# A decay chain split in two, three input products on VectorE, and new due times for the state space steps of a hybrid S5 and retention encoder

## The chip, the cores and the metric

The kernel runs on one core of a Trainium2 chip. The metric is the device time of one execution in microseconds (us); the kernel before takes 1299.02 us, the median of 3 runs (1296.56 to 1300.02).

## The reference, cut to what matters

One encoder layer is applied to two request groups, 512 and 256 positions, with 16 learned meta positions in front of each. After an RMS norm, one projection gives the inputs of two branches:

- Branch A, the state space branch (S5). For each of 2 directions, 32 groups and 64 complex states, `ab = exp(lam * dt)` is the step factor, `bb = (ab - 1) / lam * b` are the scaled input weights, `s_t = ab * s_{t-1} + bb * u_t` is the scan over positions, and `y = Re(c * s) + d * u`, then GELU and a gated projection.
- Branch B, retention with 4 heads. Its decay per head comes from `log_sigmoid(ret_decay_logit)`, 8 numbers in all, from which tables of powers of the decay are made.

The branches are merged by gates, projected and added; a second RMS norm, a gated feed-forward layer and a final RMS norm follow. The output is 512 and 256 rows of 1024.

## The kernel before, in words

**Tiling.** The 768 positions are 6 row tiles of 128, the meta positions a small seventh. Weights are split into a high and a low part (`convert`, L161: ScalarE copies the high part, `tt(eng, lo, ...)` on VectorE or POOL subtracts it), and each product is three matmuls (`mm3`, L79). Weight tiles 3 to 11 have their low parts made on POOL, the others on VectorE (L215).

**Order.** Between L590 and L1733 the order of the instructions on each engine is the order in which the program issues them. An instruction that waits holds up all that follows on its engine; the DMA queue is SyncE's (SP).

**The front (L740 to L785).** Row by row: mean square on ScalarE, `rstd_of` on POOL, `scale_row` on VectorE (L622), 8 transposes on TensorE (`to_features`, L631), high and low part (`n1_hi` on ScalarE, `n1_lo` on VectorE, L641 to L650). `u_block` (L681) projects a quarter of the S5 input for half the positions in 24 matmuls. In this row of calls stands `decay_params()` (L698 to L732, called at L775), the log-sigmoid of the 8 decays as a chain of tiny POOL operations (128x8) with one VectorE reciprocal in the middle (L718), and then `dcols` (L732), the factors that the retention tables need. `s5_params` (L435) is a generator of VectorE steps for `ab`, its powers and the scaled inputs `Bb` (`inputs`, L525 to L549, half of it three POOL operations, L541 to L543); `step(n)` runs n of them. `step(N0)` runs 11 near the start, `step(1000)` (L785) the rest.

**The lanes (L826 to L1080, L1284).** The rest of branch A is five generators:

- `e_lane`: `gbank` (L798) makes 4 groups' input matrices in 6 VectorE operations of 128x512, TensorE transposes them, multiplies by the input (L859), and ScalarE and VectorE (L863) copy the result to `X`. It works on 8 blocks, two events each, with the transposes of a block one event ahead.
- `scan_lane` (L868): 64 steps of 3 VectorE operations on `X`.
- `table_lane` (L898): for 8 blocks, `gbank` on POOL, 16 small TensorE products with `bm` (L933), and DMAs to DRAM.
- `y_lane` (L941): loads the tables, then (second event) runs whatever is left of the scan, copies `X` to `sy`, and in 9 further events does 12 matmuls per block (L985 to L987) and the GELU (L999 to L1004: ScalarE, VectorE, ScalarE, VectorE), then DMAs to DRAM.
- `ret_tables` (the retention tables) and `sums_lane` (sums of the normed input on POOL and VectorE).

**Due times.** The lanes are run between the matmuls of the plain projections (`plain_units`, L1482). The planner's clock (L1094) starts at 0 before the first of them; each piece yields its length in units: 1.92 for 12 matmuls of a `kq_unit` (L1424, 8 units of 4 pieces, to 61.44) and 1.28 for a `v_block` (L1441, 3 units of 14 pieces, to 115.2). After a piece, `passed` runs every event that is due:

```python
    events = deque(sorted(
        spread("e", *E_T, 16) + spread("r", *R_T, 64) + [(t, "s") for t in S_T] + spread("x", *X_T, 24)
        + [(T_FREE, "free")] + spread("c", T_FREE + 0.1, C_DT, 12) + spread("y", *Y_T, 12), key=lambda e: e[0]))
```

`E_T` is the start and spacing of the 16 input events, `R_T` of the 64 scan events, `S_T` the ten table events, `Y_T` the start and spacing of the output events. `v_unit` takes two weight halves before its first and two before its third piece, and each taking issues the conversion of two more (`ws.ahead = 2`, `Ops.two`).

**The end (L2347 to L2374).** Three groups of matmuls finish the lower row tiles 3, 4 and 5. After each, VectorE adds the result to `hres` (`accumulate`), `second_half` takes the mean square on ScalarE and `rstd_from` makes the scale on POOL, and `finish(i, r)` (L2272) writes two 128x512 outputs on VectorE and issues their DMAs. `finish(3)` stands after the addition of tile 4, ahead of that of tile 5.

Of the kernel before, what the change touches and what calls it, by code (L numbers as in the profile page):

```python
# [46 lines left out]
VLP = (0, 1, 2)  # L47
SEQ = 'B Z0 A D KS VM F V0 KL QD F C F F V1 F V2 KT S2 F F KU ST QL KR F F O2 S1 VL F Z2 F QU S0 O1 QR F DL Z1 QS F O0 F ZL'
HALF = 3.84
E_T = (1.9, 0.72)  # L50
R_T = (13.5, 0.997)
X_T = (45, 1.361)
S_T = (2.0, 4.8, 7.6, 10.4, 14, 20, 27, 34, 41, 48)
T_FREE = 82.607
C_DT = 2.446
Y_T = (73, 3.91)
N0 = 11


def build(nc, tc, I, O):  # L60
# [26 lines left out]
    def tt(e, out, a, b, op):  # L87
        e.tensor_tensor(out=out, in0=a, in1=b, op=op)  # L88
# [346 lines left out]
    def s5_params():  # L435
        V.memset(pw[:, 0, 0, :], 1.0)
        V.memset(pw[:, 1, 0, :], 0.0)
        dt = tmp()
        V.tensor_copy(out=dt, in_=prm[:, 2, :])
        yield  # L440
        yield from pexp(dt, G)
        lr, li = prm[:, 0, :], prm[:, 1, :]
        mag, den, dn = tmp(), tmp(), tmp()
        sincos = []

        def magnitude():
            tt(V, mag, lr, dt, MUL)
            yield
            yield from pexp(mag, G)

        def angle():
            th, k1, kf, r, zz = tmp(), tmp(), tmp(), tmp(), tmp()
            c1 = 6.28125
            c2 = 0.0019340515136718750
            c3 = 2 * math.pi - c1 - c2
            yield from chain(
                lambda: tt(V, th, li, dt, MUL),
                lambda: ts(V, k1, th, 1.0 / (2 * math.pi), MUL, MAGIC, ADD),
                lambda: ts(V, kf, k1, -MAGIC, ADD),
                lambda: stt(r, kf, -c1, th, MUL, ADD),  # L460
                lambda: stt(r, kf, -c2, r, MUL, ADD),
                lambda: stt(r, kf, -c3, r, MUL, ADD),
                lambda: ts(V, r, r, 0.25, MUL),
                lambda: tt(V, zz, r, r, MUL))
            sn, cs = tmp(), tmp()

            def sine():
                ts(V, sn, zz, 1.0 / 362880, MUL)
                yield
                for c in (-1.0 / 5040, 1.0 / 120, -1.0 / 6):  # L470
                    stt(sn, sn, c, zz, ADD, MUL)
                    yield
                stt(sn, sn, 1.0, r, ADD, MUL)
                yield

            def cosine():
                ts(V, cs, zz, -1.0 / 3628800, MUL)
                yield
                for c in (1.0 / 40320, -1.0 / 720, 1.0 / 24, -0.5):
                    stt(cs, cs, c, zz, ADD, MUL)  # L480
                    yield
                ts(V, cs, cs, 1.0, ADD)
                yield

            yield from together(sine(), cosine())
            for _ in range(2):
                s2, c2t = tmp(), tmp()
                yield from chain(
                    lambda: tt(V, c2t, sn, sn, MUL),
                    lambda: stt(s2, sn, 2.0, cs, MUL, MUL),  # L490
                    lambda: ts(V, c2t, c2t, -2.0, MUL, 1.0, ADD))
                sn, cs = s2, c2t
            sincos.extend((sn, cs))

        def denominator():
            yield from chain(
                lambda: tt(V, den, lr, lr, MUL),
                lambda: tt(V, dn, li, li, MUL),
                lambda: tt(V, den, den, dn, ADD),
                lambda: V.reciprocal(out=den, in_=den))  # L500

        yield from together(angle(), magnitude(), denominator())
        sn, cs = sincos
        tt(V, pw[:, 0, 1, :], mag, cs, MUL)
        yield
        tt(V, pw[:, 1, 1, :], mag, sn, MUL)
        yield

        def powers():
            for st, n in ((1, 1), (2, 2), (4, 4)):  # L510
                ts_ = [x0.tile([128, 4, G], F32, name="pq", tag="pq", bufs=4)[:, :n] for _ in range(4)]
                ar = pw[:, 0, st:st + 1, :].to_broadcast([128, n, G])
                ai_ = pw[:, 1, st:st + 1, :].to_broadcast([128, n, G])
                xr, xi = pw[:, 0, 1:1 + n, :], pw[:, 1, 1:1 + n, :]
                for t, a, b in zip(ts_, (xr, xi, xr, xi), (ar, ai_, ai_, ar)):
                    tt(V, t, a, b, MUL)
                    yield
                tt(V, pw[:, 0, st + 1:st + 1 + n, :], ts_[0], ts_[1], SUB)
                yield
                tt(V, pw[:, 1, st + 1:st + 1 + n, :], ts_[2], ts_[3], ADD)  # L520
                yield

        bts = [x0.tile([128, G, 16], F32, name="bt", tag="bt", bufs=2) for _ in range(2)]

        def inputs():  # L525
            t1, t2, t3, t4, cr, ci, nr = (tmp() for _ in range(7))
            ai = pw[:, 1, 1, :]
            yield from chain(
                lambda: ts(V, nr, pw[:, 0, 1, :], -1.0, ADD),
                lambda: tt(V, t2, ai, li, MUL),  # L530
                lambda: tt(V, t3, ai, lr, MUL),
                lambda: tt(V, t1, nr, lr, MUL),
                lambda: tt(V, t4, nr, li, MUL),
                lambda: tt(V, t1, t1, t2, ADD),
                lambda: tt(V, t3, t3, t4, SUB),
                lambda: tt(V, cr, t1, den, MUL),
                lambda: tt(V, ci, t3, den, MUL))
            crb = cr[:, :, None].to_broadcast([128, G, 16])
            cib = ci[:, :, None].to_broadcast([128, G, 16])
            br, bi = braw[:, 0], braw[:, 1]  # L540
            tt(P, Bb[:, 0], br, crb, MUL)  # L541
            tt(P, bts[0], bi, cib, MUL)
            tt(P, Bb[:, 0], Bb[:, 0], bts[0], SUB)  # L543
            tt(V, Bb[:, 1], bi, crb, MUL)
            yield
            tt(V, bts[1], br, cib, MUL)
            yield
            tt(V, Bb[:, 1], Bb[:, 1], bts[1], ADD)
            yield  # L549

        yield from together(inputs(), powers())
        nonlocal sc, pwE
        sc = single()
        pwE = sc.rearrange("p (r t g) -> p r t g", r=2, t=8)
        for ri in range(2):
            V.tensor_copy(out=pwE[0:64, ri], in_=pw[0:64, ri, 7::-1, :])
            yield
            V.tensor_copy(out=pwE[64:128, ri], in_=pw[64:128, ri, 0:8, :])
            yield
# [138 lines left out]
    def decay_params():  # L698
        w = [x0.tile([128, 8], F32, name=f"dp{i}") for i in range(4)]
        e, x, y, z = w  # L700
        k = x0.tile([128, 8], I32, name="dpk")
        ts(V, e, dlg, -1.0, MUL)
        tt(V, e, e, dlg, ALU.min)
        ts(P, e, e, -87.0, ALU.max)
        ts(P, x, e, 1.4426950408889634, MUL, MAGIC, ADD)
        ts(P, x, x, -MAGIC, ADD)
        for c in (-0.693359375, 2.12194440e-4):
            ts(P, y, x, c, MUL)
            tt(P, e, e, y, ADD)
        ts(P, y, e, 1.0 / 5040, MUL)  # L710
        for c in (1.0 / 720, 1.0 / 120, 1.0 / 24, 1.0 / 6, 0.5, 1.0):
            ts(P, y, y, c, ADD)
            tt(P, y, y, e, MUL)
        ts(P, k, x, 127.0, ADD, 8388608.0, MUL)
        ts(P, y, y, 1.0, ADD)
        tt(P, e, y, k.bitcast(F32), MUL)
        ts(P, z, e, 2.0, ADD)
        V.reciprocal(out=z, in_=z)  # L718
        tt(P, z, z, e, MUL)
        tt(P, x, z, z, MUL)  # L720
        ts(P, y, x, 1.0 / 17, MUL)
        for c in (15, 13, 11, 9, 7, 5, 3):
            ts(P, y, y, 1.0 / c, ADD)
            tt(P, y, y, x, MUL)
        ts(P, y, y, 1.0, ADD)
        tt(P, y, y, z, MUL)
        ts(P, y, y, -2.0, MUL)
        ts(P, x, dlg, 0.0, ALU.min)
        tt(P, lgc, y, x, ADD)
        lf, lb = lgc[:, 0:4], lgc[:, 4:8]  # L730
        for j, (src, c) in enumerate(((lf, 1.0), (lf, -1.0), (lf, 255.0), (lb, 1.0), (lb, -1.0), (lb, 256.0))):
            ts(P, dcols[:, j, :], src, c, MUL)  # L732

    params = s5_params()

    def step(n):
        for _ in range(n):
            next(params, None)
# [33 lines left out]
    scale_row(5)  # L772
    row_scale(6)
    scale_row(6)
    decay_params()  # L775
    u_block(2, 0)
    to_features(5)
    n1_hi(5)
# [3 lines left out]
    n1_lo(6)  # L782
    u_block(0, 1)
    uws[3] = ws.two()
    step(1000)  # L785
    leave(x0_cm)
    s5_cm = pool("s5")
# [1232 lines left out]
    def h21(i):  # L2020
        return hres[:, 3 + i, 0:512]
# [329 lines left out]
    for i in range(3):  # L2351
# [10 lines left out]
            finish(0, rs[0], qs=(1,))  # L2362
            finish(2, rs[2])
        if i == 1:
            finish(3, rs[3])
            tt(V, h22(2), h22(2), gfin[:, 512:], MUL)
        elif i == 2:
            tt(V, h21(2), h21(2), gfin[:, 0:512], MUL)
            finish(4, rs[4])
    yo = [row_tile() for _ in range(2)]  # L2370
# [106 lines left out]
```

## Time and profile before

| | |
|---|---|
| median of 3 runs | 1299.02 us (1296.56 to 1300.02) |
| the profiled execution | 1295.07 us |
| its span, first to last instruction | 1293.3 us |
| TensorE (PE) busy | 1207.2 us, 93% |
| VectorE (DVE) busy | 917.6 us, 71% |
| POOL busy | 680.6 us, 53% |
| ScalarE (ACT) busy | 594.2 us, 46% |
| granted TensorE clock, mean | 0.974 |
| DMA moved | 155.32 MB, queues 38.4% |

The span is 1.8 us shorter than the profiled execution, which is 3.95 us below the median. Busy shares are means over the whole program. [...]

### The profile page before, as it was taken

How to read it: one execution, taken by the hardware profiler on the slowest of the kernel's cores; microseconds unless marked ns; L12 is line 12 of the kernel's file. 1: busy time of each engine (PE TensorE's matmuls, PEld its weight loads, DVE VectorE, ACT ScalarE, POOL GpSimd, SP SyncE). 2: the span in 40 equal slices, each digit the busy share in tenths (PEclk: the TensorE clock that was granted, in tenths of full speed). 3: DMA queues.
4: the chain of work that ended last, by engine and by line, in shares of the span. 5: the costliest groups of instructions: out<-in, count | busy, mean ns of one | idle time of the engine just before them, and what ended most of it. 6: DMA issues, size and time to landing. Idle time of an engine off the chain costs nothing. (4 is left out here: it accounts for less than half of the span.)

```text
span 1293.3 us, 19211 instructions
## 1 busy us (share of the span) xinstructions
PE 1207.2 (93%) x6821; PEld 1136.7 (88%) x6821; DVE 917.6 (71%) x1514; ACT 594.2 (46%) x1242; POOL 680.6 (53%) x687
## 2 busy tenths in 40 slices
PE   7689998997998999987899997999999999999996
PEld 7688998997988989976899887999999999888884
DVE  6766996658787777887644349766666565899897
ACT  5256343634444444443433245344444444568564
POOL 4777842656676655466355028444444444564174
PEclk9889998999999999998999999999999999999998
DMA  6253456665464435244332600433322222614002
GB/s 248 50 130 100 131 185 181 157 186 168 145 200 137 148 117 182 79 149 159 126 115 74 211 17 33 125 120 94 103 90 66 79 69 78 223 66 152 12 1 97
DMA packets 76734, 155.32 MB, mean 120 GB/s; under 512 B 18000, under 2 KB 37584, under 8 KB 76640
## 3 DMA queue, kind: packets, MB, share of 16 engines
q1 hardware_dynamic: 76640, 154.11, 38.4%
q8 instruction: 53, 0.87, 0.3%
q14 instruction: 41, 0.34, 0.1%
HBM read 118.50 MB, written 35.59 MB: 119 GB/s over the span
## 5 line engine op out<-in xcount | busy, mean ns | idle before, releaser
L88 DVE TENSOR_TENSOR wlo<-wraw,whi 128x512 fp32r<-128x512 f32 x286 | 238.0, 840 | 105.3 <-ACT whi L100 105.0
L100 ACT ACTIVATE whi<-wraw 128x512 fp32r<-128x512 f32 x304 | 183.6, 623 | 46.7 <-POOL wraw L88 14.6
L88 POOL TENSOR_TENSOR wraw<-wraw 128x512 f32<-128x512 f32 x93 | 130.3, 1401 | 141.4 <-DVE wlo L88 94.6
L88 POOL TENSOR_TENSOR wraw<-wrax,wraw 128x512 f32<-128x512 f32 x38 | 51.2, 1346 | 77.4 <-DVE wlo L88 43.7
L82 PE MATMUL bank<-n1hi,wlo 128*128 128x384 f32 x192 | 66.7, 347 | 2.2 <-DVE wlo L88 2.2
L100 ACT ACTIVATE q<-bank 128x384 f32<-128x384 f32 x80 | 38.2, 484 | 66.4 <-PE bank L82 62.3
L80 PE MATMUL bank<-n1hi,whi 128*128 128x384 f32 x192 | 67.6, 352 | 0.0
L81 PE MATMUL bank<-n1lo,whi 128*128 128x384 f32 x192 | 66.4, 346 | 0.0
L80 PE MATMUL pair<-n1hi,whi 128*128 128x384 f32 (+1 forms) x168 | 61.2, 364 | 2.4 <-ACT sgst L100 2.4
L81 PE MATMUL pair<-n1lo,whi 128*128 128x384 f32 (+1 forms) x168 | 59.1, 352 | 0.0
L82 PE MATMUL pair<-n1hi,wlo 128*128 128x384 f32 (+1 forms) x168 | 59.0, 351 | 0.0
L2309 PE MATMUL acc<-whi,ahi 128*128 128x512 f32 x132 | 52.3, 396 | 0.8 <-DVE hres L88 0.8
L88 DVE TENSOR_TENSOR wlo<-wrax,whi 128x512 fp32r<-128x512 f32 x46 | 39.1, 854 | 19.3 <-ACT whi L100 19.3
L2309 PE MATMUL acc<-whi,alo 128*128 128x512 f32 x132 | 52.2, 396 | 0.0
L2309 PE MATMUL acc<-wlo,ahi 128*128 128x512 f32 x132 | 52.2, 395 | 0.0
L88 DVE TENSOR_TENSOR X<-X,single 128x128 f32<-128x128 f32 (+2 forms) x128 | 43.1, 337 | 4.4
L88 POOL TENSOR_TENSOR fr<-fr 128x384 f32<-128x384 f32 x29 | 36.2, 1253 | 13.4 <-DVE alo L88 12.9
L82 PE MATMUL bank<-yThi,wlo 128*128 128x384 f32 x128 | 43.0, 336 | 0.0
L81 PE MATMUL bank<-yTlo,whi 128*128 128x384 f32 x128 | 43.0, 336 | 0.0
L80 PE MATMUL bank<-yThi,whi 128*128 128x384 f32 x128 | 43.0, 336 | 0.0
L80 PE MATMUL pair<-whi,n1hi 128*128 128x256 f32 x144 | 41.7, 290 | 0.0
L94 POOL TENSOR_SCALAR rvar<-ss 128x1 f32<-128x1 f32 (+1 forms) x13 | 5.1, 396 | 68.6 <-ACT nx L100 68.5
(526 smaller groups left out, 4313.1 us busy)
## 6 DMA issues: line engine op xcount, KB each, us to landing
wraw<-in_wfi SPq DMA_DIRECT2D x35, 512.0 KB, 3.7
wraw<-in_win SPq DMA_DIRECT2D x33, 512.0 KB, 5.4
w<-in_wfo SPq DMA_DIRECT2D x16, 512.0 KB, 5.4
wrax<-in_win SPq DMA_DIRECT2D x11, 512.0 KB, 4.3
wrax<-in_wfi SPq DMA_DIRECT2D x11, 512.0 KB, 3.7
fb<-fbscr SPq DMA_DIRECT2D x8, 512.0 KB, 5.0
wraw<-in_wo SPq DMA_DIRECT2D x8, 512.0 KB, 3.6
ffscr<-fr SPq DMA_DIRECT2D x10, 384.0 KB, 2.9
```

The costliest lines, as they stand in the source:

```text
L80: T.matmul(out, l[0], r[0], start=start, stop=False)
L81: T.matmul(out, l[0], r[1], start=False, stop=False)
L82: T.matmul(out, l[1], r[0], start=False, stop=stop)
L88: e.tensor_tensor(out=out, in0=a, in1=b, op=op)
L94: e.tensor_scalar(out=out, in0=a, scalar1=s1, scalar2=s2, op0=op0, op1=op1)
L100: A.activation(out=out, in_=a, func=f, **kw)
L2309: T.matmul(ps, l[a], r[b], start=False, stop=False, skip_group_check=True)
```

## The change

It does four things. `decay_params` becomes a generator of two parts: the first ends before the reciprocal and stays at its place in the front; the second, with the reciprocal, follows after 62 more steps of `s5_params`, behind the first products of all four input quarters' weights. The three POOL operations of `inputs` go to VectorE, each a step of the generator. The due times of the input, scan, table and output events change: input spacing 0.72 to 1.0 units, scan start 13.5 to 18.0, tables further apart up to 57 instead of 48, output start 73 to 81.5 and spacing 3.91 to 2.8. `finish(3)` moves behind the addition of row tile 5.

```diff
-E_T = (1.9, 0.72)
-R_T = (13.5, 0.997)
+E_T = (1.9, 1.0)
+R_T = (18.0, 0.99)
 X_T = (45, 1.361)
-S_T = (2.0, 4.8, 7.6, 10.4, 14, 20, 27, 34, 41, 48)
+S_T = (2.0, 7, 13, 19.5, 26, 32.5, 39, 45.5, 52, 57)
 T_FREE = 82.607
 C_DT = 2.446
-Y_T = (73, 3.91)
+Y_T = (81.5, 2.8)
 N0 = 11
+N1 = 62
...
             br, bi = braw[:, 0], braw[:, 1]
-            tt(P, Bb[:, 0], br, crb, MUL)
-            tt(P, bts[0], bi, cib, MUL)
-            tt(P, Bb[:, 0], Bb[:, 0], bts[0], SUB)
+            tt(V, Bb[:, 0], br, crb, MUL)
+            yield
+            tt(V, bts[0], bi, cib, MUL)
+            yield
+            tt(V, Bb[:, 0], Bb[:, 0], bts[0], SUB)
+            yield
             tt(V, Bb[:, 1], bi, crb, MUL)
...
         ts(P, z, e, 2.0, ADD)
+        yield
         V.reciprocal(out=z, in_=z)
...
             ts(P, dcols[:, j, :], src, c, MUL)
+        yield
 
     params = s5_params()
+    rates = decay_params()
...
     scale_row(6)
-    decay_params()
+    next(rates)
     u_block(2, 0)
...
     u_block(0, 1)
     uws[3] = ws.two()
+    step(N1)
+    next(rates)
     step(1000)
...
         if i == 1:
-            finish(3, rs[3])
             tt(V, h22(2), h22(2), gfin[:, 512:], MUL)
         elif i == 2:
+            finish(3, rs[3])
             tt(V, h21(2), h21(2), gfin[:, 0:512], MUL)
             finish(4, rs[4])
```

## Rows read from the trace of the kernel before

**Rows 1.** Waits of PE, whole span: total us, times, longest.

```profile
PE single L638 <- DVE n1lo L88: 8.0, 1, 8.0
PE single L85 <- ACT sy L100: 4.7, 1, 4.7
PE single L832 <- DVE X L863: 2.5, 1, 2.5
PE single L832 <- ACT ks L100: 1.1, 2, 0.6
```

**Rows 2.** Timeline of DVE, 33 to 63 us: start us, us, instruction [idle before].

```profile
40.83 0.20 DVE L718 RECIPROCAL dp<-dp 128x8 f32<-128x8 f32 x1 [7.40 <-POOL dp L92]
...
49.47 1.29 DVE L88 TENSOR_TENSOR pt<-pt,prm 128x32 f32<-128x32 f32 x1
...
53.00 0.68 DVE L88 TENSOR_TENSOR Bb<-braw,pt 128x512 f32<-128x512 f32 x1
...
54.47 1.54 DVE L88 TENSOR_TENSOR Bb<-Bb,bt 128x512 f32<-128x512 f32 x1
...
62.48 0.69 DVE L88 TENSOR_TENSOR er<-er,tm 128x512 f32<-128x512 f32 x1
```

**Rows 3.** Timeline of PE, 41 to 66 us.

```profile
43.01 0.54 PE L82 MATMUL pair<-n1hi,wlo 128*128 128x400 f32 x1
...
47.34 0.48 PE L80 MATMUL pair<-n1hi,whi 128*128 128x400 f32 x1
...
63.23 0.66 PE L832 MATMUL single<-ident,er 128*128 128x128 f32 x4 [1.05 <-DVE er L88]
65.24 1.09 PE L832 MATMUL single<-ident,ei 128*128 128x128 f32 x4 [1.35 <-DVE ei L88]
```

**Rows 4.** Timeline of POOL, 47 to 56 us.

```profile
47.97 1.46 POOL L92 TENSOR_SCALAR dcols<-lgc 128x4 f32<-128x4 f32 x6
49.40 2.61 POOL L88 TENSOR_TENSOR wlo<-wrax,whi 128x512 fp32r<-128x512 f32 x2
52.78 2.69 POOL L88 TENSOR_TENSOR Bb<-braw,pt 128x512 f32<-128x512 f32 x1 [0.78 <-DVE pt L88]
```

**Rows 5.** Timeline of PE: twelve matmuls between two starts; first output product.

```profile
115.92 0.42 PE L80 MATMUL pair<-n1hi,whi 128*128 128x384 f32 x1
...
118.12 1.92 PE L85 MATMUL single<-Vt,et 128*128 128x99 f32 x16
...
214.82 1.15 PE L85 MATMUL single<-sy,fb 128*128 128x97 f32 x4 [4.74 <-ACT sy L100]
```

**Rows 6.** Stretches: us, PE busy (x) and the other engines, PEclk, DMA, GB/s.

```profile
81.70:85.10 3.40, 3.40 (x13) 3.37 (x11) 3.19 (x6) 1.20 (x3) 3.32 (x4) 0.51 1.11 244
...
214.80:222.00 7.20, 7.17 (x35) 7.18 (x35) 3.30 (x8) 4.53 (x8) 0.00 (x0) 0.53 0.59 174
```

**Rows 7.** Stretch 110 to 113 us, PE instructions with bm alone: busy (x), PEclk.

```profile
110.00:113.00 3.00, 2.16 (x16) 1.00 0.00 0
```

**Rows 8.** Timeline of DVE: first and last scan step.

```profile
121.35 0.40 DVE L88 TENSOR_TENSOR single<-X,single 64x128 f32<-64x128 f32 x1
...
212.67 0.57 DVE L88 TENSOR_TENSOR X<-X,single 128x64 f32<-128x64 f32 x2
```

**Rows 9.** Groups of DVE, 121.3 to 213.3 us: busy, mean ns, idle before.

```profile
L88 DVE TENSOR_TENSOR wlo<-wraw,whi 128x512 fp32r<-128x512 f32 x6 | 4.8, 835 | 0.0
L88 DVE TENSOR_TENSOR ks<-ks,Dg 16x64 f32<-16x64 f32 x6 | 3.8, 628 | 0.2
```

**Rows 10.** Stretch 222 to 262 us: PE, PEld, DVE, ACT, POOL busy, PEclk.

```profile
222.00:262.00 40.00, 40.00 (x348) 39.86 (x347) 23.39 (x41) 24.29 (x44) 22.84 (x21) 1.00 0.70 180
```

**Rows 11.** Timelines of DVE and POOL at the end.

```profile
1284.58 0.68 DVE L88 TENSOR_TENSOR hres<-acc,hres 128x512 f32<-128x512 f32 x1
...
1284.97 0.27 POOL L94 TENSOR_SCALAR rstd<-rtmp,rstd 128x1 f32<-128x1 f32 x1
1286.17 0.76 POOL L94 TENSOR_SCALAR rvar<-fss 128x1 f32<-128x1 f32 x1 [0.93 <-ACT yo L100]
```

## The prediction

> **What bounds the kernel now.** The span is 1293.3 us and PE is busy for 93% of it, so I read the waits of PE first: the reader is to see how short they are beside the span, and that those of 8.0, 4.7 and 2.5 us lead to code that the change touches [rows 1]. Then I looked up, in the timelines of the engine named, why it was late.
>
> The largest, 8.0 us, is one wait for a low part `n1lo`. VectorE stood 7.40 us before the reciprocal of `decay_params`, because POOL was working through the tiny operations ahead of it [rows 2]; the `n1lo` behind it were ready to run, and PE needed them. PE paid twice: after the wait its clock was at the lower level. From 43.01 to 47.34 us 13 matmuls start 0.333 us apart [rows 3]; at the full clock twelve take 2.20 us, 0.183 each [rows 5]. Sixteen at the slow pace cost another 2.4 us. The same is seen after the wait of 2.5 us (the stretch at clock 0.51) and after that of 4.7 us (0.53) [rows 6].
>
> Later VectorE bounds: its scan runs from 121.35 to 213.24 us [rows 8] almost without a gap, with only 6 `wlo` and 6 `ks` operations (8.6 us) between the steps [rows 9], and PE stands 4.7 us for the `sy` copied from its result [rows 1].
>
> **The change, part by part.**
>
> *Decay chain.* VectorE no longer waits at its old place, so `n1lo` and all behind it come about 7.5 us earlier (the wait and the reciprocal's issue), and PE gets the wait of 8.0 and the 2.4 us back: 10.4 us at the end of the next four projections. The reciprocal, 62 steps further, waits for nothing: POOL ends the first part at about 40.8 us as before, VectorE arrives some 3 us after that. The second part on POOL, up to `dcols` at 47.97+1.46 [rows 4], some 8 us, moves to about 44 to 53 us; what it gives is needed at unit 45. Queued behind it on POOL are the low parts of the fifth weight tile (55 us), needed near 64: that slack covers it; without it the price would be those 8 us.
>
> *Inputs on VectorE.* Three operations of 0.68 us [rows 2], 0.65 to the next start: 1.9 us more on VectorE. They take away three POOL operations beside which VectorE was held: its `Bb` operation took 1.54 us beside POOL's of 2.69, 0.86 more than the 0.68 alone [rows 2, 4]. I count 0.86 for each of the three, 2.6 us. The step chain so ends 7.5 - 1.9 - 0.1 + 2.6 = 8.1 us earlier. Against that, POOL's two conversions (2.61 us [rows 4]) now fall beside `gbank` of the first block. Bounds: nothing, as in `er<-er,tm`, 0.69 us beside POOL's scaling of `Cc` [rows 2]; or 1.1 us for each of its two operations with both inputs in SBUF, as for the `pt` operation that took 1.29 beside the same conversions [rows 2, 4] where its neighbours take 0.18. I take 0.7, nearer to the row of the same size and kind.
> [...]
>
> *What is late next.* PE must wait for `er` and `ei` before the fourth quarter's second half: 1.05 and 1.35 us now [rows 3]. PE comes 10.4 us earlier, they come 8.1 - 0.7 = 7.4 earlier, so this wait grows by 3.0. The front is worth 7.4 us, less 0.8 for a slow stretch about twice as long as the 0.9 us that the six slow matmuls there cost now: **6.6 us**, between 5.1 (2.2 for contention) and 8.1.
>
> *Input events.* At 0.72 units three of them came due after one piece: transposes, products, transposes; the second transposes found their PSUM banks not yet copied out (2.5 us [rows 1]), and the slow clock after it cost half of 3.4 us [rows 6]. At 1.0 units it is one pair per 12 matmuls. The two `ks` waits (1.1 us [rows 1]) go to wider table spacing. Of 5.3 us I leave 1.0: **4.3 us**, between 0 and 5.3.
>
> *Scan, tables and outputs.* All due before unit 81.92 (16 input events, the table products) is the same work for PE in another order, so PE reaches it 6.6 + 4.3 = 10.9 us earlier, at 199.2 us where it was at 210.1 (214.82 less the wait of 4.74 [rows 5]). The last input event moves from unit 13.44 to 17.28: two groups of 12 matmuls more before it (4.4 us [rows 5]), one table set less (2.16 us [rows 7]). The scan therefore begins 10.9 - 2.2 = 8.7 us earlier, at 112.65. The third and fourth weight halves of the second `v_unit` are converted in VectorE's queue behind 62 of the 64 steps, since the scan now ends at unit 80.4 and these are issued at 79.36. Before, the scan's 91.9 us lay ahead of them; now 91.9 - 2.1 (two steps) + 0.6 (one more `ks` [rows 9]) + 0.7 (the first half): the first low part is there at 203.7. PE needs it at 199.2: a wait of 4.5 us for `wlo` takes the place of the 4.7 us for `sy`, with the same slow clock. By the time `sy` is due (unit 88.32, 7.7 us of PE work later) it is ready. **0**, between +8.1 (no wait, no slow clock: 4.7 and half of 7.2) and -2.
>
> *Output events* come every 2.8 units, about 5.9 us with their products, for 6.9 before. PE had no wait there; ScalarE was busy 24.29 of 40 us and VectorE 23.39 [rows 10], 70% at the new pace. 0, down to -4. On SP's queue the table and output DMAs move past weight loads issued several pieces ahead of their use: covered by that lead, else the price is a `wlo` wait as above.
>
> *End.* The addition of tile 5 starts at 1284.58 [rows 11] behind `finish(3)`. Now it runs as soon as PE's last product is there, but POOL is in the scale of tile 4 until 1285.24, so tile 5's starts there instead of at 1286.17 [rows 11]: **0.9 us**, between 0 and 1.4. `finish(3)` and its two DMAs fit in VectorE's and SP's idle time before the last scale.
>
> **Sum.** 6.6 + 4.3 + 0 + 0 + 0.9 = 11.8 us. The profiled execution (1295.07 us) would take 1283.3. It lies 3.95 us below the median of 1299.02, which I take as the base: 1287.2.
>
> **Rivals.**
> 1. *POOL holds up the front.* The contention term at its full 2.2 and the `ks`/PSUM waits back (0 instead of 4.3): 5.1 + 0.9 = 6, 1293. For: the 1.29 us row. Against: `er<-er,tm`. It differs from the forecast in the wait for `ei`. Chance 0.14. [...]
> 2. *The wait at 81.92 goes too.* If VectorE is a few us faster, PE needs no `wlo` wait and keeps its clock: up to 8.1 more, 1279. For: VectorE is the only cause; against: the count above. 0.14.
> 3. *The output events become the bound, and it is slower.* A GELU passes ScalarE, VectorE, ScalarE, VectorE in order beside the `sy` copies, sums and weights. If that chain can't be done in 5.9 us, each of the 8 spacings of L1004 falls back to 6.9 (8 us) and PE's clock drops after each wait, as behind all waits over 2 us here: half of 3.4 us, 8 times, 13.6. Net 11.8 - 21.6 = 9.8 slower, 1309. It decides from 2 us of lag per event on. Against: 70% busy. 0.08.
> 4. *It comes to nothing:* VectorE stays the bound through the scan, and the earlier front only makes PE wait longer at 81.92: 1298. This needs the scan to begin no earlier, and [rows 8] show it starting right behind the last input event. 0.09.
>
> **How the numbers follow.** The forecast has 0.55 and gives 1287.2. 1279 to 1296.5 takes in rivals 1 and 2 and leaves out rival 3 and most of 4, some 2 in 10 with the forecast's own edges; the forecast's own range is 1283 to 1292. The limit of 0.3% is 3.9 us, about what a measurement can tell. Faster: forecast, rival 2 and most of 1, 0.81; the same: the rest of 1 and most of 4, 0.11; slower: 0.08.
>
> **What would show it.** Right: no `n1lo` wait over 1 us and clock 1.0 from 35 to 50 us; waits for `er`, `ei` of some 4 and 1.4 us near 52 to 58; no 2.5 us wait at L832 later; the scan beginning near 112; a wait for `wlo` near 199 and none for `sy`; the last addition of a row tile some 10 us before the span's end (8.7 now). Wrong: waits of PE between 205 and 255 us (rival 3), a scan beginning after 116 (rivals 1, 4), or a new wait after 280 us, where nothing was changed.

## The result, and the profile after

The kernel after takes 1281.95 us, the median of 4 runs (1278.82 to 1285.09); the kernel before, run beside it, 1297.79 us (1290.01 to 1300.02). The ratio is 0.9889, with a 95% interval of 0.9839 to 0.9938: 14 us faster, between 8 and 21. The forecast was 1287.2, in a range of 1279.0 to 1296.5. Medians take in every run; the ratios of this document leave out two executions far above all others, 1439.1 us of the kernel before and 4111.85 us of h_both.

| | before | after |
|---|---|---|
| the profiled execution | 1295.07 us | 1285.09 us |
| its span | 1293.3 us | 1283.1 us |
| PE busy | 1207.2 us, 93% | 1206.8 us, 94% |
| VectorE busy | 917.6 us, 71% | 915.6 us, 71% |
| POOL busy | 680.6 us, 53% | 675.5 us, 53% |
| granted TensorE clock, mean | 0.974 | 0.973 |

PE does the same work; what changed is what it waits for. Lines in the kernel after stand 1 to 9 higher than before (the transposes of the lanes are at L841, `X` is copied at L872, `tt` at L89). First the waits of PE in the kernel after, 20 to 260 us, to be held against [rows 1] (total us, times, longest):

```profile
PE pair L82 <- DVE wlo L89: 3.9, 1, 3.9
...
PE single L86 <- ACT ks L101: 2.1, 1, 2.1
...
PE single L841 <- DVE er L89: 0.9, 1, 0.9
PE single L642 <- DVE n1lo L89: 0.4, 1, 0.4
```

The waits of 8.0 us for `n1lo`, 4.7 for `sy` and 2.5 for `X` are gone or below 0.5. Two have come in: 3.9 us for `wlo` and 2.1 us for `ks`; this `ks` wait is another than the two of [rows 1], which stood before transposes and are gone. The places, in the timeline of PE in the kernel after (start us, us, instruction, idle time before and what ended it), which answers to [rows 3] and [rows 5]:

```profile
35.61 0.39 PE L642 MATMUL single<-ident,nx 16*128 16x16 f32 x4 [0.70 <-DVE dp L93]
...
56.94 0.65 PE L841 MATMUL single<-ident,er 128*128 128x128 f32 x4 [0.86 <-DVE er L89]
58.95 1.09 PE L841 MATMUL single<-ident,ei 128*128 128x128 f32 x4 [1.36 <-DVE ei L89]
...
86.25 0.72 PE L86 MATMUL single<-fr,bm 128*48 128x144 f32 x2 [2.10 <-ACT ks L101]
...
207.11 0.58 PE L82 MATMUL pair<-wlo,n1hi 128*128 128x256 f32 x1 [3.90 <-DVE wlo L89]
```

The first row is the landmark of all that follows: the transposes of the first meta tile. The code up to it is the same in all kernels, yet the twelve profiles reach it between 33.16 and 35.61 us (33.30 in that of before, 35.61 here), so stages are compared by the time from there. **A** is the time from the landmark to the transposes of `ei`, the end of the front: 58.95 - 35.61 = 23.34 us, against 31.94 before. **B** is the time from the landmark to the first product named `bank<-whi,n1hi`, which is issued when the due events are over (274.37 us in the profile of before, 265.95 in that of after): 230.34 us, against 241.07.

The timeline of VectorE in the kernel after shows what became of [rows 2] and [rows 8]:

```profile
43.56 1.29 DVE L89 TENSOR_TENSOR pq<-pw 128x32 f32<-128x32 f32 x1
44.78 1.33 DVE L89 TENSOR_TENSOR pt<-pw,prm 128x32 f32<-128x32 f32 x1
...
46.95 0.19 DVE L723 RECIPROCAL dp<-dp 128x8 f32<-128x8 f32 x1
...
56.19 0.69 DVE L89 TENSOR_TENSOR er<-er,tm 128x512 f32<-128x512 f32 x1
...
60.04 1.01 DVE L89 TENSOR_TENSOR er<-er,tm 128x512 f32<-128x512 f32 x1
...
115.68 0.39 DVE L89 TENSOR_TENSOR single<-X,single 64x128 f32<-64x128 f32 x1
...
206.38 1.28 DVE L89 TENSOR_TENSOR wlo<-wrax,whi 128x512 fp32r<-128x512 f32 x2
...
1271.98 0.68 DVE L89 TENSOR_TENSOR hres<-acc,hres 128x512 f32<-128x512 f32 x1
...
1278.86 0.48 DVE L93 TENSOR_SCALAR yq<-hres,rstd 128x512 f32<-128x512 f32 x1 [0.93 <-POOL rstd L95]
```

The reciprocal waits for nothing, where it stood 7.40 us. Row seven is the low part that PE stands for at 207.11, still behind VectorE's scan steps; row eight is the addition of tile 4. And POOL in the kernel after, which answers to [rows 4]:

```profile
43.50 2.56 POOL L89 TENSOR_TENSOR wlo<-wrax,whi 128x512 fp32r<-128x512 f32 x2
47.22 0.28 POOL L89 TENSOR_TENSOR dp<-dp,dp 128x8 f32<-128x8 f32 x1 [1.16 <-DVE pt L89]
...
50.08 0.69 POOL L93 TENSOR_SCALAR dp<-dp 128x8 f32<-128x8 f32 x1
...
53.58 0.23 POOL L93 TENSOR_SCALAR dp<-dp 128x8 f32<-128x8 f32 x1
...
57.35 1.90 POOL L93 TENSOR_SCALAR dcols<-lgc 128x4 f32<-128x4 f32 x6
59.23 2.96 POOL L89 TENSOR_TENSOR wlo<-wraw,whi 128x512 fp32r<-128x512 f32 x2
```

The second part of the decay chain runs from 47.22 to 59.25 us. Its operations of eight columns take 0.69 us beside VectorE's `Bb` and `bt`, which have 512 columns and both inputs in SBUF, and 0.23 later, also beside `er<-single,Bb` (from 54.87 us), which has 512 columns too but one input in PSUM.

Last, stretches of the kernel after (us, PE, PEld, VectorE, ScalarE, POOL busy, granted clock, DMA, GB/s), against [rows 6]. The granted clock is 1.00 or 0.50 at every moment of both profiles, and 0.50 is the lower clock of this text. Behind each of the two new waits PE is at it:

```profile
86.10:89.50 3.40, 3.25 (x12) 2.63 (x13) 2.95 (x5) 1.15 (x4) 0.88 (x2) 0.52 0.00 0
205.60:212.40 6.80, 5.29 (x25) 5.29 (x25) 5.37 (x15) 1.49 (x2) 0.00 (x0) 0.51 1.02 290
```

What the lower clock costs is an estimate wherever it is counted below: half of the time that PE works in such a stretch. In the kernel after, ten matmuls of 400 columns start 0.333 us apart from 38.53 us on, at the lower clock, and the five from 42.07 us on 0.182 apart, so that half is a little high (0.151 of 0.333 is 45%).

**The ledger of the one profiled pair.** To the end of the front 31.94 - 23.34 = 8.6 us. From there to the end of the due events (241.07 - 31.94) - (230.34 - 23.34) = 2.1. Behind that 1.8, of which 1.2 is the end: from the addition of tile 4 to VectorE's last scaling it takes 6.88 us after (1271.98 to 1278.86 above) and 8.08 before, in these rows of VectorE in the kernel before:

```profile
1280.98 0.68 DVE L88 TENSOR_TENSOR hres<-acc,hres 128x512 f32<-128x512 f32 x1
...
1289.06 0.49 DVE L92 TENSOR_SCALAR yq<-hres,rstd 128x512 f32<-128x512 f32 x1 [0.93 <-POOL rstd L94]
```

The other 0.6 was not traced. In all 12.5 us; the after profile gives back 2.3 of it by reaching the landmark later, so the spans differ by 10.2.

### The profile page after: what moved, and what is told of

It reads as the page before. It is cut to its first block, busy times and chain, and to the rows that moved or that the text cites. A ratio compares the mean times of both kernels' runs of the same rounds, so it can differ in the third digit from the quotient of the medians.

```text
span 1283.1 us, 19207 instructions
## 1 busy us (share of the span) xinstructions
PE 1206.8 (94%) x6821; PEld 1136.1 (89%) x6821; DVE 915.6 (71%) x1517; ACT 594.9 (46%) x1242; POOL 675.5 (53%) x684
## 4 chain that ended last, share of the span: by engine, by line
PE 46%; DVE 4%; POOL 3%; issue 3%; ACT 2%; DMA 0%; POOLq 0%; DVEq 0%; ACTq 0%
PE bank L1141 15%; PE bank L83 7%; PE bank L81 7%; PE bank L82 7%; PE acc L2318 5%; PE acc L81 2%; PE acc L82 2%; PE acc L83 2%; DVE wlo L89 1%; POOL xc L89 1%; DVE alo L89 1%; POOL rstd L89 0%; ACT whi L101 0%; DMA wraw<-in_wglu 0%; DVE hres L89 0%
## 5 line engine op out<-in xcount | busy, mean ns | idle before, releaser
L89 DVE TENSOR_TENSOR wlo<-wraw,whi 128x512 fp32r<-128x512 f32 x286 | 236.4, 834 | 106.7 <-ACT whi L101 106.4
L89 POOL TENSOR_TENSOR wraw<-wraw 128x512 f32<-128x512 f32 x93 | 130.1, 1399 | 141.8 <-DVE wlo L89 94.8
L89 POOL TENSOR_TENSOR wraw<-wrax,wraw 128x512 f32<-128x512 f32 x38 | 51.1, 1345 | 77.7 <-DVE wlo L89 44.0
L89 DVE TENSOR_TENSOR wlo<-wrax,whi 128x512 fp32r<-128x512 f32 x46 | 38.8, 848 | 17.2 <-ACT whi L101 17.2
L89 DVE TENSOR_TENSOR X<-X,single 128x128 f32<-128x128 f32 (+2 forms) x128 | 43.0, 336 | 4.4
L82 PE MATMUL pair<-wlo,n1hi 128*128 128x256 f32 x144 | 41.8, 290 | 3.9 <-DVE wlo L89 3.9
L89 POOL TENSOR_TENSOR fr<-fr 128x384 f32<-128x384 f32 x29 | 36.1, 1253 | 13.4 <-DVE alo L89 12.9
```

Source lines behind the costliest of these rows:

```text
L82: T.matmul(out, l[0], r[1], start=False, stop=False)
```

## The experiments

All ten, with A and B from their profiles. The ratio is to the kernel before on the same chip.

| kernel | median us | ratio, 95% interval | A us | B us |
|---|---|---|---|---|
| before | 1297.79 | 1 | 31.94 | 241.07 |
| after | 1281.95 | 0.9889 [0.9839, 0.9938] | 23.34 | 230.34 |
| a_split | 1293.15 | 0.9979 [0.9959, 0.9999] | 29.52 | 238.16 |
| b_front | 1284.91 | 0.9925 [0.9904, 0.9945] | 23.33 | 231.44 |
| c_spacing | 1293.54 | 0.9987 [0.9968, 1.0006] | 32.08 | 239.60 |
| d_inputs | 1292.97 | 0.9982 [0.9964, 1.0000] | 31.04 | 237.59 |
| e_no_inputs | 1289.25 | 0.9951 [0.9930, 0.9972] | 29.58 | 236.51 |
| f_pool_weights | 1277.47 | 0.9857 [0.9826, 0.9888] | 23.35 | 225.61 |
| g_tables | 1278.01 | 0.9867 [0.9843, 0.9891] | 23.36 | 223.41 |
| h_both | 1274.39 | 0.9835 [0.9810, 0.9861] | 23.35 | 223.54 |
| i_end | 1292.59 | 0.9976 [0.9950, 1.0002] | 34.54 | 242.63 |
| j_tile3 | 1275.72 | 0.9853 [0.9821, 0.9885] | 26.30 | 225.90 |

### The front: two edits that are worth more together

**a_split**: before, with the decay chain in two parts alone.

```diff
+N1 = 62
...
+        yield
         V.reciprocal(out=z, in_=z)
...
-    decay_params()
+    next(rates)
...
+    step(N1)
+    next(rates)
     step(1000)
```

> The kernel before with the decay chain in two parts and nothing else; the three input operations (br by cr, bi by ci, their difference) stay on POOL. My theory: the two edits of the front are not independent. POOL's three operations now stand in its queue behind the second part of the decay chain (12 us of POOL in the run of after), so the ei that the second transposes want come late: the wait of 8.0 us for n1lo is gone, a wait of some 4 to 6 us for er or Bb takes its place, and the time is 1 to 5 us below the kernel before (interval from the first meta tile's transposes to the transposes of ei, 31.9 us before and 23.3 after, here 27 to 31). Rival: the parts are independent, as my sum counted them: then the split alone gives 7.5 to 10 us, interval 22 to 24.5.

A fell by 2.4 us only, and PE stood 8.6 us for `er`. The timeline of VectorE in this kernel names what it waited for:

```profile
59.34 0.69 DVE L89 TENSOR_TENSOR er<-single,Bb 128x512 f32<-128x512 f32 x1 [7.14 <-POOL Bb L89]
```

and that of POOL shows why `Bb` was late:

```profile
54.57 1.35 POOL L93 TENSOR_SCALAR dcols<-lgc 128x4 f32<-128x4 f32 x6
...
58.04 1.26 POOL L89 TENSOR_TENSOR Bb<-Bb,bt 128x512 f32<-128x512 f32 x1
```

The moved half of the decay chain stands on POOL right in front of the three input operations. The wait of 7.4 us on VectorE is not removed but moved some 17 us on, where `er` pays 7.1. The dependence of the two edits is shown.

**d_inputs**: before, with the inputs on VectorE alone.

```diff
-            tt(P, Bb[:, 0], br, crb, MUL)
-            tt(P, bts[0], bi, cib, MUL)
-            tt(P, Bb[:, 0], Bb[:, 0], bts[0], SUB)
+            tt(V, Bb[:, 0], br, crb, MUL)
+            yield
+            tt(V, bts[0], bi, cib, MUL)
+            yield
+            tt(V, Bb[:, 0], Bb[:, 0], bts[0], SUB)
+            yield
```

> The kernel before with the three input operations on VectorE and nothing else. My theory: VectorE has 1.9 us more to do, and 2.6 us come back because POOL no longer reads beside its Bb operations: 0.7 us faster, within -1 to 2, interval from the first meta tile's transposes to the transposes of ei about 31.2 us (31.9 before). Rival: contention is not what makes those operations long, and the 1.9 us are simply added: 1.9 us slower, interval 33.8.

A fell by 0.9. On VectorE in this kernel the operation that took 1.54 us beside POOL [rows 2] is back to the time of its neighbours:

```profile
55.80 0.67 DVE L88 TENSOR_TENSOR Bb<-Bb,bt 128x512 f32<-128x512 f32 x1
```

So three operations were added to the busiest chain and it became shorter. It is these rows that show it: A alone is not so exact, since the unedited front takes 31.94, 32.08 and 34.54 us in the profiles of before, c_spacing and i_end. The rest of the fall of B (3.5 us) goes with no wait that changed but with the lower clock, and is not shown to be of the edit. One stretch of it, 31 to 35 us behind the landmark in the profile of before, is missing here, of which 1.4 us lay beyond A. Another begins 3 us before PE's wait for `sy` ends (clock 0.51 from 211.0 to 213.9 us), so that PE works in it for 4.0 us and not for 6.9, which is 1.4 us less. The two make the 2.6.

**b_front**: both edits, nothing else.

> The kernel before with the decay chain in two parts and the three input operations on VectorE; tables, scan and output steps and the end as before. My theory: the whole gain of the front, 8.3 us by the traces (7 to 10), interval from the first meta tile's transposes to the transposes of ei 23.3 us. The input events then still carry the wait X of 2.5 us and unit 81.92 the wait for sy of 4.7 us. Rival: what the front gains is given back where the scan begins (VectorE bounds there, and the wait for sy grows by what is gained): then under 4 us.

A 23.33 us, 8.6 below before, where the two alone gave 2.4 + 0.9 = 3.3. The ratio says 9.7 us (7.1 to 12.4). PE still stands 2.5 us for `X` and 4.75 for `sy` in this kernel, so nothing of the front's gain is given back at the scan. B falls by 9.6, 1.0 more than A. Behind the wait for `X`, which ends at 73.41 us, PE keeps its clock in this kernel, where 3.4 us at the lower one followed in before (1.7 us less):

```profile
70.00:90.00 20.00, 17.21 (x131) 16.18 (x131) 14.35 (x27) 14.93 (x43) 19.61 (x20) 1.00 0.62 127
```

Behind `ei` it works longer at the lower clock than before, which takes 0.9 of that back.

**e_no_inputs**: after, with the three input operations back on POOL.

> The kernel after with the three input operations back on POOL. My theory: they queue behind the second part of the decay chain on POOL; er and ei come 3 to 7 us later and PE waits for them, with a lower clock behind it: 3 to 7 us slower than after, interval from the first meta tile's transposes to the transposes of ei 27 to 31 us (23.3 after). Rival, the sum of the prediction, which gave the move of the inputs 0.7 us: no more than 1 us slower than after, interval 24.

The same from the other side: A 6.2 and B 6.2 us above after, with PE's waits in this kernel led by

```profile
PE single L838 <- DVE er L89: 7.2, 1, 7.2
```

Without the inputs' edit the front would have kept little more than a quarter of its gain (2.4 of 8.6 us).

### The due times

**c_spacing**: before, with the four new tables of due times alone.

```diff
-E_T = (1.9, 0.72)
-R_T = (13.5, 0.997)
+E_T = (1.9, 1.0)
+R_T = (18.0, 0.99)
...
-S_T = (2.0, 4.8, 7.6, 10.4, 14, 20, 27, 34, 41, 48)
+S_T = (2.0, 7, 13, 19.5, 26, 32.5, 39, 45.5, 52, 57)
...
-Y_T = (73, 3.91)
+Y_T = (81.5, 2.8)
```

> The kernel before with the four new spacings (E_T, R_T, S_T, Y_T) alone. My theory from the trace of after: 0.9 us at the input events, where a wait for ks takes the place of that for X, and 1.6 us at unit 81.92, where a wait of 3.9 us for wlo takes the place of that of 4.7 us for sy: 2.5 us faster (0.5 to 4). Rival, as my sum counted it: 4.3 us at the input events and nothing at unit 81.92: 3.5 to 5.5 us. Third: the new waits are those of the earlier front alone, and without it the spacings give 6 us or more.

B fell by 1.5 us; the ratio alone (1.7 us, -0.8 to 4.1) would not tell it from nothing. Waits of PE in this kernel:

```profile
PE pair L81 <- DVE wlo L88: 5.2, 1, 5.2
...
PE single L85 <- ACT ks L100: 2.1, 1, 2.1
```

The waits for `X` (2.5), `sy` (4.7) and twice for `ks` (1.1) went, and these came in their place. They belong to the new due times, not to the earlier front.

**g_tables**: after, with other table events.

```diff
-S_T = (2.0, 7, 13, 19.5, 26, 32.5, 39, 45.5, 52, 57)
+S_T = (2.0, 11, 16.5, 21.5, 27, 33, 39, 45.5, 52, 57)
```

> The kernel after with the ten table events at (2.0, 11, 16.5, 21.5, 27, 33, 39, 45.5, 52, 57) in place of (2.0, 7, 13, 19.5, 26, 32.5, 39, 45.5, 52, 57). My theory: the wait of 2.1 us for ks comes because the second table event falls right behind two input events, whose copies stand before its own on ACT; moved by 4 units it meets no such pair, and the wait and the lower clock behind it (3.3 us at 86 to 89.5 us of after) are gone: 2 to 4 us faster than after. Rival: the wait belongs to the PSUM bank or to the table event itself, wherever it stands: the wait for ks turns up later and the time is within 1 us of after.

The second table event moves from unit 7 to 11, the next four by 0.5 to 3.5 units. The wait for `ks` does not come again at any table event, and B is 6.9 us below after. In this kernel's stretches PE keeps its clock where the second table event now stands:

```profile
85.00:95.00 10.00, 9.64 (x71) 9.01 (x71) 9.74 (x18) 7.65 (x22) 7.44 (x7) 1.00 0.01 2
```

The reason that I had given for the wait is not borne out. At unit 11 too the second table event falls right behind two input events, as PE in this kernel shows (the products of an input event, then the two halves of the table's):

```profile
89.02 1.93 PE L86 MATMUL single<-Vt,et 128*128 128x99 f32 x16
90.87 0.45 PE L86 MATMUL single<-fr,bm 128*48 128x144 f32 x2
...
92.41 0.45 PE L86 MATMUL single<-fr,bm 128*48 128x144 f32 x2 [0.36 <-DVE X L872]
```

In the kernel after the third table event does so as well (input products at 101.54 us, the table's at 103.40) and PE does not wait. That the wait hangs on the times of the table events is shown: it is 2.1 us in after, c_spacing, e_no_inputs and f_pool_weights, and gone in the three kernels with the new times. What it was about unit 7 stays open.

The waits show a part beyond my 2 to 4 us:

```profile
PE pair L82 <- DVE wlo L89: 2.7, 1, 2.7
```

The wait for `wlo` is 1.2 us shorter, and PE works 3.1 us at the lower clock behind it and not 5.3 (1.0 less). Why was not tried. Another part goes with code that no edit touched. The same stretch behind `ei`, first in after and then in this kernel, is:

```profile
59.00:62.40 3.40, 3.40 (x12) 3.38 (x13) 3.33 (x6) 0.70 (x2) 3.40 (x5) 0.51 0.81 269
59.00:62.40 3.40, 3.40 (x21) 3.40 (x22) 3.33 (x6) 0.70 (x2) 3.40 (x5) 1.00 0.67 250
```

That is 1.7 us. The sum is 2.1 for `ks` and 1.6 for the clock behind it, 1.2 and 1.0 at `wlo`, and these 1.7, in all 7.6; 0.4 more of short waits and 0.4 that was not traced leave the 6.9. The medians differ by 3.9 us, less than their intervals can tell.

**f_pool_weights**: after, with the low parts of weight tiles 12 to 15 on POOL.

```diff
-            yield from plain(i, P if 3 <= i < 12 else V)
+            yield from plain(i, P if 3 <= i < 16 else V)
```

> The kernel after with the low parts of weight tiles 12 to 15 on POOL, as those of tiles 3 to 11 are, and no longer on VectorE. My theory: at unit 81.92 wlo is late because it stands among VectorE's scan steps; on POOL it comes in time, the wait of 3.9 us and the slow clock behind it are gone, and VectorE's scan ends some 4 to 5 us earlier: 3 to 7 us faster than after. Rival: sy, which VectorE's scan and ACT's copies give, is late at the same unit and takes the wait's place: within 1 us of after. Third: POOL is the later engine there (2.6 to 3.0 us for each conversion) and PE waits for wlo still: slower than after by up to 3 us.

No wait for `wlo` is left, none for `sy` has come, and the clock stays up. This kernel's stretch at unit 81.92:

```profile
200.00:212.00 12.00, 11.21 (x94) 10.87 (x92) 10.14 (x21) 6.98 (x13) 10.29 (x9) 1.00 0.88 227
```

B is 4.7 us below after: VectorE's queue was the cause of this wait, and POOL had the room (in the kernel after it is busy for 0.00 of the 6.80 us from 205.6). The medians differ by 4.5 us, with intervals of the ratios that overlap.

**h_both**: f_pool_weights and g_tables together.

> The kernel after with the table events and the weight tiles of the two runs before it together. My theory: both gains add, 5 to 10 us faster than after. Rival: with PE earlier by the one, VectorE or POOL becomes late for the other: no more than the larger of the two.

The fastest kernel of the study: 1274.39 us, a ratio of 0.9835 to before. By B it is no better than g_tables alone (223.54 and 223.41); the median is 3.6 us lower, with intervals of the ratios that overlap. The longest waits of PE before the end of B, beside the five short ones for `sgst`, are:

```profile
PE single L841 <- DVE er L89: 2.4, 1, 2.4
PE single L86 <- DMA fb<-fbscr: 1.4, 2, 0.8
```

A new wait stands in for the one removed: the tables that come back from DRAM (`fb`) are now the last thing that the output events want. B hides a part: from 54.9 to 61.7 us the granted clock is 0.50 in this profile, which costs PE 2.5 us behind `ei`, where g_tables ran at 1.00. Without that B would be some 2 us below g_tables, by my estimate from these figures. How much of the two gains adds stays open.

### The end, and the price of POOL beside VectorE

**i_end**: before, with `finish(3)` behind the addition of tile 5 and nothing else.

```diff
         if i == 1:
-            finish(3, rs[3])
             tt(V, h22(2), h22(2), gfin[:, 512:], MUL)
         elif i == 2:
+            finish(3, rs[3])
```

> The kernel before with the output of the fourth row tile moved behind the addition to the third half, and nothing else. My theory: from the addition that gives the last tile to VectorE's last scaling 6.9 us in place of 8.1, 1.2 us faster, which the median alone can hardly tell from nothing. Rival: the work of the fourth tile now stands before that of the last one on POOL, and the last tile's chain pays for it: 0 to 2 us slower, and an end stretch of 8.1 us or more.

On VectorE, first a row of the front, then the addition of tile 4 and the last scaling:

```profile
58.83 4.20 DVE L88 TENSOR_TENSOR pq<-pw 128x128 f32<-128x128 f32 x4
...
1284.55 0.68 DVE L88 TENSOR_TENSOR hres<-acc,hres 128x512 f32<-128x512 f32 x1
...
1291.43 0.48 DVE L92 TENSOR_SCALAR yq<-hres,rstd 128x512 f32<-128x512 f32 x1 [0.93 <-POOL rstd L94]
```

From 1284.55 to 1291.43 it is 6.88 us, to the hundredth what the kernel after takes, and 1.2 less than before. The median cannot tell it from nothing, as expected. The same profile had something else to show: A is 34.54 us, with the front of before in which nothing was changed. The first row above is part of it; beside it POOL of this kernel has

```profile
60.24 2.64 POOL L88 TENSOR_TENSOR wlo<-wraw,whi 128x512 fp32r<-128x512 f32 x2
```

The same two in the profile of before are:

```profile
56.94 1.98 DVE L88 TENSOR_TENSOR pq<-pw 128x128 f32<-128x128 f32 x4
59.23 2.55 POOL L88 TENSOR_TENSOR wlo<-wraw,whi 128x512 fp32r<-128x512 f32 x2 [0.87 <-ACT whi L100]
```

There POOL's conversion waited 0.87 us for its input and began 2.3 us behind the start of the four `pq` operations, which took 1.98 us. Here it did not wait, began 1.4 us behind their start, and they took 4.20.

**j_tile3**: h_both, with the low parts of weight tile 3 on VectorE too.

```diff
-            yield from plain(i, P if 3 <= i < 16 else V)
+            yield from plain(i, P if 4 <= i < 16 else V)
```

> The kernel with the table events and the weight tiles changed, and the low parts of weight tile 3 on VectorE too, not on POOL. My theory: the two operations of 32 columns that take 1.3 us each, beside POOL's conversions of that tile, shrink to the 0.18 us of their neighbours; two conversions of 0.68 us on VectorE take the place: the interval from the first meta tile's transposes to the transposes of ei falls from 23.3 to some 22.4 us, and the time by 0 to 1 us. Rival: what makes these two operations long is not POOL's reading; then the two conversions are simply added and the interval is 24.6 us, up to 1.4 us slower.

VectorE in this kernel:

```profile
38.89 0.70 DVE L89 TENSOR_TENSOR wlo<-wrax,whi 128x512 fp32r<-128x512 f32 x1 [2.46 <-ACT whi L101]
41.07 0.69 DVE L89 TENSOR_TENSOR wlo<-wrax,whi 128x512 fp32r<-128x512 f32 x1 [1.48 <-ACT whi L101]
...
47.86 0.18 DVE L89 TENSOR_TENSOR pt<-pw,prm 128x32 f32<-128x32 f32 x1
```

Both theories missed A (26.30 us), yet the cause of the long `pq` and `pt` is settled: with no conversion on POOL beside them all take 0.18 us, where two took 1.29 and 1.33 in the kernel after. What I had left out is that VectorE must now itself wait for ScalarE's high part, 2.46 and 1.48 us. The sum closes: 3.94 of waits, 1.2 for two conversions of 0.6 from start to start, less 2.2 for `pq` and `pt`, is 2.9; A rose by 2.95. The exchange costs: B is 2.4 us above that of h_both. The medians, 1275.72 and 1274.39 us, do not tell the two apart.

In these runs each of the two engines holds up the other: `pt` takes 1.33 us beside POOL's conversion and 0.18 where that is moved away, and POOL's decay operations take 0.69 us beside VectorE's `Bb` and `bt` and 0.23 later. On whether it matters which of the two begins first, i_end alone bears, one profile in which POOL's conversion came earlier and VectorE's operations took longer (4.20 us, not 1.98).

## Why the prediction was right, and where it was not

The sum was 11.8 us, and the profiled pair shows 12.5 from the landmark on. The sign, the time's range and most places were right. That the sum came out so near is luck in part: the front gave almost 2 us more than forecast, the input events 2.7 less, and unit 81.92 gave 1.6 where nothing was forecast. The median, 1281.95 us, lies below the 1283 to 1292 that the prediction gave as the forecast's own range.

*Front: forecast 6.6, measured 8.6.* The mechanism was right: the wait for `n1lo` went from 8.0 to 0.4 us, the reciprocal waits for nothing, and A is 23.3 us in all five kernels that have the front of after (the table). The size fell short by the two deductions. The 0.8 for a longer slow stretch concerns matmuls behind the end of A. In b_front it came as counted: twelve slow ones (57.23 to 61.35 us) in place of six (65.97 to 68.12), 0.9 us. In the kernel after there were eight (59.69 to 62.45), 0.3 us, so that the front is worth 8.3 there. One sign failed here, the clock of 1.0 from 35 to 50 us: PE is ahead of VectorE, and in the kernel after it spends part of that slack at the lower clock (0.50 from 38.5 to 41.9 us) and waits 0.9 us for `er`, not 4. In b_front, f_pool_weights and h_both it keeps the full clock until there and waits 2.4; A is the same. The 0.7 for contention beside the first block was misplaced: the decay's second part took 12 us, not 8, so POOL's conversions came at 59.23, beside the second block. `er<-er,tm` is 0.69 in the first and 1.01 in the second. The chain itself came 8.6 us earlier where 8.1 were counted. Of that 0.5, 0.3 is the inputs (2.8 us of contention less 1.8 of work, where 2.6 less 1.9 was counted). The rest lies ahead of them: `pw` starts 15.3 us behind the landmark before and 7.6 after, 7.7 us where 7.5 was counted.

*What the front's parts are worth.* Here the reasoning held only for the whole. The step "Inputs on VectorE" gave that edit 2.6 - 1.9 = 0.7 us. Alone it measured 0.9 (the contention removed was not three times 0.86 but 0.86 on `Bb`, 0.86 on the `pw` and 1.1 on the four `pq` behind it, 2.8 in all); with the split in place, 6.2 (A of e_no_inputs less A of after). The prediction listed what is queued on POOL behind the second part as the low parts of the fifth weight tile, which is true only because the input operations are no longer there; it did not say that this is what the second edit is for.

*Input events: forecast 4.3, measured 1.6. This is the step that failed.* It put at 1.0 us what would be left of the waits for `X` and `ks` and their slow clock, 5.3 in all. The waits that it named went, the two for `ks` too. But a new one came for which the 1.0 had no room: 2.1 us for `ks` between the two halves of the second table event, with 3.4 us at the lower clock behind it (1.6 lost), so that 3.7 was left. The new times that were to spread the waits made this one, since c_spacing has it without the earlier front, and other table times (g_tables) took it away. Why unit 7 has it and unit 11 not is open. From the front's end to the end of the due events the kernel after gained 2.1 us, and c_spacing, without the front, 1.6: some 1.6 here and 1.6 at unit 81.92, less 0.3 behind `ei` and 0.6 for one more short wait for `sgst`.

*Unit 81.92: forecast 0, measured 1.6.* A wait of 4.5 us for `wlo` in place of 4.7 for `sy` was forecast; 3.9 us was measured, in a stretch of lower clock of 6.8 us that began 1.5 us before the wait ended, so that PE worked in it for 5.3 us and not 6.9 as before. That is 1.6 us gained. The count of what stands before it on VectorE was right, and f_pool_weights shows that this queue was all of the cause.

*Outputs: forecast 0.* No wait of PE over 0.6 us stands from 212 to 260 us; rival 3 fell. *End: forecast 0.9, measured 1.2.*

*The rivals.* The full contention (1) did not come at the front (`er<-er,tm` of the first block 0.69 us, as before), rival 2 did not come by itself but is what f_pool_weights makes. Rival 3 priced its waits by what the profile of before shows, the lower clock behind each of twelve waits over 2 us (2.42 to 7.96); b_front has a wait of 2.5 us for `X` behind which the clock stays at 1.00. Rivals 3 and 4 are excluded by PE's waits and by the scan's start (115.68 us, 113.4 on the clock of before; forecast 112.65).

The base, 1299.02, was a median of three runs; beside the later kernels before took 1295 us. This moves the time in microseconds, not the difference.

## What to carry to other kernels

A chain that is moved behind other work takes its place in a queue, and all that stood in that queue behind the new place is now behind it: look for what is wanted next on that engine and move it off in the same edit, or the wait only changes its name (VectorE's 7.40 us before the reciprocal became 7.14 before `er` in a_split). Judge such edits together, not one by one: here the two gave 0.9 and 2.4 us alone and 8.6 together. When waits are spread by due times, new ones can come in: here the wider spacing took away 3.6 us of waits and brought one of 2.1. Read from the trace after which event now waits, and move that one; neither the mean spacing nor the count of events that meet in one piece of work showed it.

## What the runs showed of the hardware that was not expected

*The same matmuls at two paces.* From the first product named `mx1hi` to the first named `ahi`, code that no edit touched, the profiles of a_split, c_spacing and d_inputs take 403.3 to 403.5 us and the other nine 408.7 to 409.0. PE waits for nothing between 820 and 1080 us and the granted clock is 1.00 in both. The groups of PE in that stretch (busy us, mean ns), first of before:

```profile
L80 PE MATMUL bank<-n22hi,whi 128*128 128x384 f32 x72 | 24.4, 339 | 0.0
```

then of a_split:

```profile
L81 PE MATMUL bank<-n22hi,whi 128*128 128x384 f32 x72 | 24.2, 336 | 0.0
```

These 5.5 us are more than most edits of this study are worth. No kernel was profiled twice, but the twelve times of c_spacing lie in two groups, 1289.4 to 1291.8 and 1295.3 to 1297.9 us, as if they came and went from one execution to the next. The cause was not tried; the three profiles were taken on one chip, on which b_front took 408.7. It is why the stages are compared by A and B, which end ahead of this stretch.

*A lower clock that falls in other places.* The kernels with the front of after run the same code to its end, but PE is at the lower clock from 38.5 to 41.9 and from 59.0 to 62.4 us in after, from 37.8 to 41.0 in g_tables, only from 58.3 to 61.8 in f_pool_weights, and from 54 to 62 in b_front and h_both. Ahead of `er` this costs slack alone; behind `ei` it costs from nothing (g_tables) to 2.5 us (h_both). So B, other than A, carries some 2 us that no edit made.

*An unchanged front, 2.6 us longer.* In i_end A is 34.54 us, in before 31.94. POOL's conversion came 0.9 us earlier against VectorE's four `pq` operations, and these took 4.20 us and not 1.98. That the one made the other is my reading of one profile; it was not tried.
